# Scores, transposes and values of an attention part as bursts, the first score held until two banks are free

## The chip, the cores and the metric

The kernel runs on one core of a Trainium2 chip. The metric is the device time of one execution in microseconds, as the median of several runs.

## The reference

Two blocks of layers over a sequence of 256 rows of 1024 features, all in float32. The first block has two layers of a hybrid mixer (attention beside a state-space branch) and a feed-forward part. The second has four layers, each of two feed-forward parts around a mixer: sliding-window attention with sinks, attention with three branches, block attention, sliding-window attention again. Every mixer has attention of this form:

```python
s = jnp.einsum("bqgrd,bkgd->bgrqk", q_n, k_n).astype(jnp.float32) * scale + bias
p = masked_softmax(s, ok, sink)
o = jnp.einsum("bgrqk,bkgd->bqgrd", p.astype(v.dtype), v_n)
```

Heads have 64 features. Queries and keys stand in blocks of 128 rows; the later block sees both blocks of keys, the earlier one only its own.

## The kernel before

The 256 rows are two tiles of 128, t = 0 and t = 1. Weights stream from HBM, are split into a rounded part and a remainder by ScalarE and VectorE (lines 192, 193, 197, 198), and TensorE multiplies with three products each (lines 227 to 229 for projections, 245 to 247 for products with the rows of an output weight).

All attention goes through `attend`. It takes eight heads in two parts of four. The four heads of a part are named by `par` (0 or 1) and `i` (0 or 1); `par` says in which half of the 128 partitions the head's 64 features lie. A part does the following.

- Scores, line 638: a matmul of 64 rows for each `i`, each block of keys `kt` (one for t = 0, two for t = 1) and each `par`. The heads of `par` 0 go to the PSUM tile `s[0]`, those of `par` 1 to `s[1]`. Each takes a bank of the pool `acc`, which has two banks for each t. The same pool holds the projections of the mixers (`proj`) and the sums of the output product (`acc`), so a new `s` needs both banks of its t back from whatever stood there.
- Reductions with the bias on VectorE (line 646), exponentials on ScalarE (line 649), the divisor (lines 653 to 658), the scaling of the weights of attention (lines 660 and 661).
- Transposes of the attention weights on TensorE (line 669), four to a bank: for t = 0 one bank holds both `par`, for t = 1 each `par` has its own. A copy brings them to SBUF (line 672 on VectorE or 674 on ScalarE).
- Values, line 680: matmuls of 64 columns, `par` 0 to the upper half of the partitions of one bank, `par` 1 to the lower.

The order of the instructions on each engine isn't that of the program text. A scheduler takes, for each engine, the instruction of the lowest priority number among those that it finds ready, by its own estimates; the engines then work their lists in order, with semaphores between them. Numbers go up by one with each instruction, and `pr` sets where a block of work begins: the second tile's work lies `lag` units of weights behind the first's. So the matmuls of lines 638, 669 and 680 are mixed with projections and output products wherever their banks or operands come free one by one.

Six stretches of the program have attention: the hybrid layers (two parts for each t), the two sliding-window mixers and the block mixer C (four), and the mixer B with its two branches of full attention (eight).

Of the kernel before, what the change touches and what calls it, by code (L numbers as in the profile page):

```python
# [17 lines left out]
P = 128  # L18
# [83 lines left out]
class Program:  # L102
# [29 lines left out]
    @contextmanager  # L132
    def pr(self, t, first=0):


        tc = self.tc
        at = int(1000 * (self.unit + {0: 0, 1: self.lag, 2: -PREP}[t] - first))
        key = t, first
        keep, tc.cur_priority = tc.cur_priority, 20000 + max(at, self.at.get(key, 0))
        try:  # L140
            yield
        finally:
            self.at[key] = tc.cur_priority - 20000
            tc.cur_priority = keep

    def btile(self, t, shape, dtype=F32, name="b"):
        return self.wp.tile(shape, dtype, name=f"{name}{t}", tag=f"b{t}", bufs=NB)
# [475 lines left out]
    def attend(self, t, q, k, v, bias, out, sink=None, gate=None, parts=(0, 1)):  # L623

        nc = self.nc
        nk = (t + 1) * P
        four = lambda a: a.rearrange("p (i r) -> p r i", r=2)
        for part in parts:  # L630
            heads = slice(4 * part, 4 * part + 4)
            m, den, rden = (self.small(t, [P, 2, 2], n) for n in ("m", "den", "rden"))
            s = [self.acc(t, (P, 2, 256), "s") for _ in range(2)]
            for i in range(2):
                for kt in range(t + 1):
                    for par in range(2):
                        h = 4 * part + par + 2 * i
                        nc.tensor.matmul(s[par][:, i, kt * P:(kt + 1) * P], q[64 * par:64 * par + 64, h // 2],  # L638
                                         k(h, kt), start=True, stop=True)
            e = [self.btile(t, [P, 2, 256], name="e") for _ in range(2)]  # L640
            for par in range(2):
                for i in range(2):
                    h = 4 * part + par + 2 * i
                    ei = e[par][:, i, :nk]
                    init = BIG if sink is None else sink[1][:, h:h + 1]
                    nc.vector.tensor_tensor_reduce(
                        out=ei, in0=s[par][:, i, :nk], in1=bias(h)[:, 256 - nk:256], scale=-0.125,
                        scalar=init, op0=OP.add, op1=OP.min, accum_out=m[:, par, i:i + 1])
                    nc.scalar.activation(ei, ei, AF.Exp, scale=-1.0, bias=m[:, par, i:i + 1],
                                         accum_out=den[:, par, i:i + 1])  # L650
            if sink is not None:
                z = self.small(t, [P, 2, 2], "sk")
                nc.vector.tensor_add(z, four(sink[0][:, heads]), m)
                nc.scalar.activation(z, z, AF.Exp)
                nc.vector.tensor_add(den, den, z)
            nc.vector.reciprocal(rden, den)
            if gate is not None:
                nc.vector.tensor_mul(rden, rden, four(gate[:, heads]))
            for i in range(2):
                nc.scalar.activation(e[0][:, i, :nk], e[0][:, i, :nk], AF.Identity, scale=rden[:, 0, i:i + 1])  # L660
            nc.vector.tensor_mul(e[1][:, :, :nk], e[1][:, :, :nk], rden[:, 1, :, None].to_broadcast([P, 2, nk]))
            pts = {}
            step = 2 - t
            for par in range(0, 2, step):
                tp = self.bank(t, (P, step, 2, t + 1, P), "tp")
                for r in range(step):
                    for i in range(2):
                        for kt in range(t + 1):
                            nc.tensor.transpose(tp[:, r, i, kt], e[par + r][:, i, kt * P:(kt + 1) * P], self.ident)  # L669
                pt = self.wp.tile([P, step, 2, t + 1, P], F32, name=f"pt{t}", tag=f"pt{t}", bufs=2)  # L670
                if (par if t else part):
                    nc.vector.tensor_copy(pt, tp)
                else:
                    nc.scalar.activation(pt, tp, AF.Copy)
                pts.update({par + r: pt[:, r] for r in range(step)})
            pv = self.bank(t, (P, 2, P), "pv")
            for i in range(2):
                for kt in range(t + 1):
                    for par in range(2):
                        nc.tensor.matmul(pv[64 * par:64 * par + 64, i], v(4 * part + par + 2 * i, kt),  # L680
                                         pts[par][:, i, kt], start=(kt == 0), stop=(kt == t))
            out(part, pv)

    def stationary(self, t, tag="X", n=4):
# [233 lines left out]
    def do_B(self, i, j):  # L918
# [19 lines left out]
        def c():  # L938
            Wc = self.columns(W, [(1024, 512)])
            for u in range(2):  # L940
                pr = self.btile(0, [16, P], name="pr")
                nc.sync.dma_start(pr, A["b_cmp_pos_2"][j, u].rearrange("(k i) d -> k (i d)", i=2))
                tp = self.bank(0, (P, 16), "tp")
                nc.tensor.transpose(tp, pr, self.ident[:16, :16])
                ptile = bp.tile([P, 16], F32, name=f"pos{u}")
                nc.vector.tensor_copy(ptile, tp)
                pos.append(ptile)
                w = bp.tile([P, 2, 2, 64], F32, name=f"cw{u}")
                for e in range(2):
                    nc.sync.dma_start(w[:, :, e], A["b_cmp_w2_2"][j, u].rearrange("(k p) n -> p k n", p=P))  # L950
                w2.append(w)
            for t in range(NT):
                with self.pr(t):
                    ps = self.project(t, X[t], Wc, 512)
                    for u in range(2):
                        self.compress_source(t, ps[:, u * 256:(u + 1) * 256], raw[:, u])
# [350 lines left out]
```

## Time and profile before

| | |
|---|---|
| median of 3 runs | 2733.43 us (2732.55 to 2736.84) |
| the profiled execution | 2739.28 us, span 2737.5 us |
| TensorE busy | 2673.5 us, 98% |
| VectorE busy | 1796.9 us, 66% |
| ScalarE busy | 1547.4 us, 57% |
| GpSimd busy | 96.3 us, 4% |
| granted TensorE clock, mean | 0.995 |

Busy time of TensorE is the time in which at least one matmul is under way; matmuls overlap, and their ends are modelled. How much of the engine's time a matmul takes is therefore read from the starts of rows that follow each other. The chain of work that ended last lies on TensorE for 79% of the span. A matmul with full float32 operands, such as those of lines 638 and 680, leaves two records, a transpose and a projection one.

### The profile page before, as it was taken

How to read it: one execution, taken by the hardware profiler on the slowest of the kernel's cores; microseconds unless marked ns; L12 is line 12 of the kernel's file. 1: busy time of each engine (PE TensorE's matmuls, PEld its weight loads, DVE VectorE, ACT ScalarE, POOL GpSimd, SP SyncE). 2: the span in 40 equal slices, each digit the busy share in tenths (PEclk: the TensorE clock that was granted, in tenths of full speed). 3: DMA queues.
4: the chain of work that ended last, by engine and by line, in shares of the span. 5: the costliest groups of instructions: out<-in, count | busy, mean ns of one | idle time of the engine just before them, and what ended most of it. 6: DMA issues, size and time to landing. Idle time of an engine off the chain costs nothing.

```text
span 2737.5 us, 36688 instructions
## 1 busy us (share of the span) xinstructions
PE 2673.5 (98%) x12883; PEld 2141.6 (78%) x12883; DVE 1796.9 (66%) x3466; ACT 1547.4 (57%) x2893; POOL 96.3 (4%) x102
## 2 busy tenths in 40 slices
PE   8999999999999999999999999999999999999998
PEld 6678787778788778878877778788777788887787
DVE  8866668776665676576557766666566656657764
ACT  6645546565554565565455655555576555547653
POOL 0300002100000000000000000000000000000000
PEclk9999999999999999999999999999999999999999
DMA  6357742566566346555552266565546656553662
GB/s 208 102 165 207 214 131 88 172 218 188 179 190 195 117 161 203 189 185 185 184 185 81 80 213 188 175 199 185 162 139 187 200 175 196 189 166 112 208 192 85
DMA packets 338277, 465.18 MB, mean 170 GB/s; under 512 B 27780, under 2 KB 273196, under 8 KB 338092
## 3 DMA queue, kind: packets, MB, share of 16 engines
q1 hardware_dynamic: 336512, 460.49, 53.8%
q10 hardware_dynamic: 1580, 2.35, 0.5%
q8 instruction: 101, 1.65, 0.3%
q14 instruction: 84, 0.69, 0.1%
HBM read 460.13 MB, written 2.62 MB: 169 GB/s over the span
## 4 chain that ended last, share of the span: by engine, by line
PE 79%; DVE 8%; DMA 6%; ACT 3%; issue 2%; POOL 1%; SPq 0%; ACTq 0%; DVEq 0%; POOLq 0%
PE proj L227 15%; PE proj L229 15%; PE proj L228 15%; PE acc L245 8%; PE acc L247 8%; PE acc L246 8%; PE s L638 3%; DMA stage<-in_ffn_w_in 2%; PE tp L254 2%; DVE slot L198 2%; DVE slot L193 2%; PE pv L680 2%; DMA stage<-in_w_up 2%; PE tp L669 1%; ACT slot L197 1%
## 5 line engine op out<-in xcount | busy, mean ns | idle before, releaser
L198 DVE SCALAR_TENSOR_TENSOR slot<-stage,gt,slot 128x512 fp32r<-128x512 f32 (+2 forms) x1024 | 710.4, 740 | 339.7 <-ACT slot L197 338.8
L197 ACT ACTIVATE slot<-stage,gt 128x512 fp32r<-128x512 f32 (+2 forms) x1024 | 677.2, 710 | 409.8 <-PE proj L229 199.7
L227 PE MATMUL proj<-slot,X 128*128 128x512 f32 (+2 forms) x2272 | 897.2, 395 | 10.7 <-DVE X L257 8.8
L229 PE MATMUL proj<-slot,X 128*128 128x512 f32 (+2 forms) x2272 | 883.3, 389 | 0.0
L228 PE MATMUL proj<-slot,X 128*128 128x512 f32 (+2 forms) x2272 | 882.5, 388 | 0.0
L227 PEld LDWEIGHTS proj<-slot,X 128*128 128x128 f32 x2272 | 428.1, 189 | 101.7 <-DVE X L257 13.0
L229 PEld LDWEIGHTS proj<-slot,X 128*128 128x128 f32 x2272 | 428.0, 188 | 86.5 <-issue 0.9
L193 DVE TENSOR_TENSOR slot<-stage,slot 128x1024 fp32r<-128x1024 f32 (+1 forms) x330 | 406.6, 1235 | 134.5 <-ACT slot L192 131.2
L228 PEld LDWEIGHTS proj<-slot,X 128*128 128x128 f32 x2272 | 428.9, 189 | 79.8 <-issue 1.3
L192 ACT ACTIVATE slot<-stage 128x1024 fp32r<-128x1024 f32 (+1 forms) x330 | 346.9, 1054 | 166.7 <-DMA stage<-in_ffn_w_out 66.0
L245 PE MATMUL acc<-slot,H 128*128 128x512 f32 x880 | 353.5, 402 | 4.6 <-ACT H L256 4.6
L247 PE MATMUL acc<-slot,H 128*128 128x512 f32 x880 | 344.3, 392 | 1.8 <-DVE H L257 1.7
L246 PE MATMUL acc<-slot,H 128*128 128x512 f32 x880 | 343.3, 390 | 0.0
L504 ACT ACTIVATE th<-proj,r 128x256 f32<-128x256 f32 x220 | 103.7, 472 | 296.7 <-PE proj L229 273.9
L506 DVE SCALAR_TENSOR_TENSOR h<-th,proj 128x256 f32<-128x256 f32 x220 | 91.8, 417 | 208.5 <-ACT th L504 208.4
L247 PEld LDWEIGHTS acc<-slot,H 128*128 128x128 f32 x880 | 165.1, 188 | 41.4 <-DVE H L257 5.8
L245 PEld LDWEIGHTS acc<-slot,H 128*128 128x128 f32 x880 | 165.3, 188 | 39.6 <-ACT H L256 9.2
L246 PEld LDWEIGHTS acc<-slot,H 128*128 128x128 f32 x880 | 165.7, 188 | 31.5
L257 DVE TENSOR_TENSOR H<-tp,H 128x256 fp32r<-128x256 f32 x220 | 92.1, 419 | 33.2 <-ACT H L256 32.8
L256 ACT ACTIVATE H<-tp 128x256 fp32r<-128x256 f32 x220 | 83.0, 377 | 39.6 <-PE tp L254 39.5
L507 DVE SCALAR_TENSOR_TENSOR h<-h,r,proj 128x256 f32<-128x256 f32 x220 | 104.0, 473 | 0.7
L278 POOL TENSOR_TENSOR rstd<-rstd,mhalf 128x1 f32<-128x1 f32 x34 | 29.1, 855 | 2130.8 <-DVE rstd L273 2067.7
(219 smaller groups left out, 2169.5 us busy)
## 6 DMA issues: line engine op xcount, KB each, us to landing
stage<-in_ffn_w_in SPq DMA_DIRECT2D x704, 256.0 KB, 3.9
stage<-in_ffn_w_out SPq DMA_DIRECT2D x176, 512.0 KB, 4.1
stage<-in_w_in SPq DMA_DIRECT2D x48, 512.0 KB, 3.8
stage<-in_w_gate SPq DMA_DIRECT2D x88, 256.0 KB, 3.8
stage<-in_w_up SPq DMA_DIRECT2D x88, 256.0 KB, 4.0
stage<-in_w_down SPq DMA_DIRECT2D x44, 512.0 KB, 4.5
stage<-in_w_out SPq DMA_DIRECT2D x24, 512.0 KB, 3.7
stage<-in_c_w_in SPq DMA_DIRECT2D x24, 512.0 KB, 4.4
```

What stands on the lines that cost most here:

```text
L192: nc.scalar.activation(r[:, 0], s[:, i:i + step], AF.Copy)
L193: nc.vector.tensor_sub(r[:, 1], s[:, i:i + step], r[:, 0].bitcast(F32))
L197: nc.scalar.activation(r[:, 0, j], s[:, i + j], AF.Identity, scale=gk)
L198: nc.vector.scalar_tensor_tensor(r[:, 1, j], s[:, i + j], gk, r[:, 0, j].bitcast(F32), op0=OP.mult, op1=OP.subtract)
L227: mm(ps, x[0], w[1], start=start, stop=False)
L228: mm(ps, x[0], w[0], start=False, stop=False)
L229: mm(ps, x[1], w[0], start=False, stop=stop)
L245: mm(acc[j], a[0], wl, start=start and i == 0, stop=False)
L246: mm(acc[j], a[0], wh, start=False, stop=False)
L247: mm(acc[j], a[1], wh, start=False, stop=stop and i == n - 1)
L504: nc.scalar.activation(th, pg[:, 0:256], AF.Tanh, scale=self.r_half[t])
L507: nc.vector.scalar_tensor_tensor(h, h, self.r_square[t], pg[:, 256:512], op0=OP.mult, op1=OP.mult)
```

## The change

`burst` emits a list of calls. The first keeps its place in the order of priorities and may depend on an instruction given as `after`; the others get numbers lower by 10000 and are bound to program order, so that they follow the first as soon as the scheduler finds them ready. It is used for the scores, the transposes and the values.

For the scores, a memset of one element of `s[1]` on VectorE is made first, and the first score, which writes `s[0]`, depends on it. The memset itself can only run when the bank of `s[1]` is free. The scores' loop changes from `i, kt, par` to `kt` (falling), `i, par`. The transposes of t = 0 begin with `par` 1. In the values, `par` 1 comes ahead of `par` 0, so that the first value is one that needs the copy made last.

```diff
+    def burst(self, calls, after=None):
+        tc = self.tc
+        keep = tc.cur_priority
+        for i, (f, args, kw) in enumerate(calls):
+            ins = f(*args, **kw)
+            if i == 0:
+                if after is not None:
+                    tc.add_manual_dep(ins.ins, after.ins.name, mybir.DependencyInfo(
+                        mybir.DependencyClass.Sync, mybir.DependencyReason.DATA), reason="both banks")
+                tc.cur_priority -= 10000
+            else:
+                tc.keep_in_program_order(ins)
+        tc.cur_priority = keep + len(calls)
...
             s = [self.acc(t, (P, 2, 256), "s") for _ in range(2)]
-            for i in range(2):
-                for kt in range(t + 1):
-                    for par in range(2):
-                        h = 4 * part + par + 2 * i
-                        nc.tensor.matmul(s[par][:, i, kt * P:(kt + 1) * P], q[64 * par:64 * par + 64, h // 2],
-                                         k(h, kt), start=True, stop=True)
+            held = nc.vector.memset(s[1][0:1, 0, 0:1], 0.0)
+            self.burst([(nc.tensor.matmul, (s[par][:, i, kt * P:(kt + 1) * P],
+                                            q[64 * par:64 * par + 64, 2 * part + i], k(4 * part + par + 2 * i, kt)),
+                         dict(start=True, stop=True))
+                        for kt in range(t, -1, -1) for i in range(2) for par in range(2)], held)
...
-                for r in range(step):
-                    for i in range(2):
-                        for kt in range(t + 1):
-                            nc.tensor.transpose(tp[:, r, i, kt], e[par + r][:, i, kt * P:(kt + 1) * P], self.ident)
+                self.burst([(nc.tensor.transpose, (tp[:, r, i, kt], e[par + r][:, i, kt * P:(kt + 1) * P],
+                                                   self.ident), {})
+                            for r in range(step - 1, -1, -1) for i in range(2) for kt in range(t + 1)])
...
-            for i in range(2):
-                for kt in range(t + 1):
-                    for par in range(2):
-                        nc.tensor.matmul(pv[64 * par:64 * par + 64, i], v(4 * part + par + 2 * i, kt),
-                                         pts[par][:, i, kt], start=(kt == 0), stop=(kt == t))
+            self.burst([(nc.tensor.matmul, (pv[64 * par:64 * par + 64, i], v(4 * part + par + 2 * i, kt),
+                                            pts[par][:, i, kt]), dict(start=(kt == 0), stop=(kt == t)))
+                        for i in range(2) for kt in range(t + 1) for par in (1, 0)])
```

In the rows of the order below, the number behind a name tells its tiles apart. TensorE's order at the first scores of t = 1 in the first sliding-window mixer, before: `s1_8447` is `s[0]` of the first part and `s1_8448` its `s[1]`, `s1_8503` is `s[0]` of the next part, and `proj1` and `tp1` belong to a projection of the same tile.

```order
L229 MATMUL proj1_8327<-slot_8289,X1_8062 128x512
L638 MATMUL s1_8447<-slot_8084,slot_8085 128x128
L638 MATMUL s1_8447<-slot_8085 128x128
L638 MATMUL s1_8447<-slot_8084,slot_8085 128x128
L638 MATMUL s1_8447<-slot_8085 128x128
L265 MATMUL tp1_8354<-c1_81,cp1_8352 128x128 x4
L638 MATMUL s1_8448<-slot_8084,slot_8085 128x128
L638 MATMUL s1_8448<-slot_8085 128x128
L638 MATMUL s1_8448<-slot_8084,slot_8085 128x128
L638 MATMUL s1_8448<-slot_8085 128x128
L638 MATMUL s1_8503<-slot_8084,slot_8085 128x128
```

The same place of TensorE's order now, where `s1_8457` and `s1_8458` are the two banks of the first part:

```order
L280 MATMUL tp1_8362<-c1_81,cp1_8360 128x128 x4
L151 MATMUL s1_8457<-slot_8093 128x128
L151 MATMUL s1_8458<-slot_8093 128x128
L151 MATMUL s1_8457<-slot_8093 128x128
L151 MATMUL s1_8458<-slot_8093 128x128
L151 MATMUL s1_8457<-slot_8092,slot_8093 128x128
L151 MATMUL s1_8458<-slot_8092,slot_8093 128x128
L151 MATMUL s1_8457<-slot_8092,slot_8093 128x128
L151 MATMUL s1_8458<-slot_8092,slot_8093 128x128
L262 MATMUL acc0_8808<-slot_8770,X0_8568 128x512
```

The four scores of one bank and, behind a transpose, the four of the other have become one run of eight that alternates between the banks, and the next part's scores no longer stand behind it.

TensorE's order at the values of the second part of t = 1, a little later in the same mixer, before (`acc0` is the output product of the other tile, `pt1` the copied transposes):

```order
L246 MATMUL acc0_8792<-slot_8764,X0_8556 128x512
L680 MATMUL pv1_8545<-pt1_8536,slot_8084 64x128
L247 MATMUL acc0_8792<-slot_8764,X0_8556 128x512
L245 MATMUL acc0_8793<-slot_8764,X0_8556 128x512
L680 MATMUL pv1_8545<-pt1_8543,slot_8084 64x128
L680 MATMUL pv1_8545<-pt1_8536,slot_8085 64x128
L680 MATMUL pv1_8545<-pt1_8543,slot_8085 64x128
L680 MATMUL pv1_8545<-pt1_8536,slot_8084 64x128
L680 MATMUL pv1_8545<-pt1_8543,slot_8084 64x128
L680 MATMUL pv1_8545<-pt1_8536,slot_8085 64x128
L680 MATMUL pv1_8545<-pt1_8543,slot_8085 64x128
L246 MATMUL acc0_8793<-slot_8764,X0_8556 128x512
```

The values of the same part now, with the last score of a later part ahead of them:

```order
L151 MATMUL s1_8715<-slot_8092,slot_8093 128x128
L151 MATMUL pv1_8557<-pt1_8555,slot_8092 64x128
L151 MATMUL pv1_8557<-pt1_8548,slot_8092 64x128
L151 MATMUL pv1_8557<-pt1_8555,slot_8093 64x128
L151 MATMUL pv1_8557<-pt1_8548,slot_8093 64x128
L151 MATMUL pv1_8557<-pt1_8555,slot_8092 64x128
L151 MATMUL pv1_8557<-pt1_8548,slot_8092 64x128
L151 MATMUL pv1_8557<-pt1_8555,slot_8093 64x128
L151 MATMUL pv1_8557<-pt1_8548,slot_8093 64x128
L261 MATMUL acc0_8808<-slot_8795,X0_8368 128x512
```

The lone value and the seven behind two output products have become one run of eight.

VectorE's order in the same mixer, around the first part's reductions of t = 1, now (`e1`, `m1`, `sk1` and `den1` are the part's own, `slot` and `stage` are weights):

```order
L660 ISA e1_8469,m1_8454<-s1_8458,bias_8078,nsink_8090 128x256
L660 ISA m1_8454 128x1
L649 MEMSET s1_8515 1x1
L208 TENSOR_TENSOR slot_8800<-stage_8798,slot_8800 128x1024
L667 TENSOR_TENSOR sk1_8478<-sink_8088,m1_8454 128x4
L208 TENSOR_TENSOR slot_8805<-stage_8803,slot_8805 128x1024
L669 TENSOR_TENSOR den1_8455<-den1_8455,sk1_8478 128x4
L660 ISA e1_8525,m1_8511<-s1_8514,bias_8078,nsink_8090 128x256
```

The memset of the next part stands right behind the last reduction of this part; before, the next part's first reduction stood there, with its scores already made.

## Rows read from the trace of the kernel before

**Rows 1.** Page: busy us (share of the span) and instructions of each engine.

```profile
PE 2673.5 (98%) x12883; PEld 2141.6 (78%) x12883; DVE 1796.9 (66%) x3466; ACT 1547.4 (57%) x2893; POOL 96.3 (4%) x102
```

**Rows 2.** Stretches, length, then busy PE, PEld, DVE, ACT, POOL (instructions); clock, DMA.

```profile
1468.00:1551.00 83.00, 82.78 (x607) 61.66 (x607) 62.39 (x235) 59.62 (x189) 0.00 (x0) 1.00 0.15 46
934.00:990.00 56.00, 55.92 (x358) 41.09 (x357) 39.20 (x127) 40.68 (x121) 0.00 (x0) 1.00 0.32 103
2008.00:2060.00 52.00, 51.96 (x346) 39.02 (x345) 33.13 (x106) 37.15 (x107) 0.00 (x0) 1.00 0.36 111
...
57.00:111.00 54.00, 49.69 (x283) 36.35 (x281) 49.31 (x123) 38.03 (x91) 16.80 (x13) 1.00 0.31 93
415.00:469.00 54.00, 49.85 (x290) 36.82 (x288) 49.54 (x123) 38.34 (x90) 16.08 (x13) 1.00 0.30 92
```

**Rows 3.** Waits of PE, 55 to 112 us: us in total, times, longest.

```profile
PE s L638 <- DVE m L646: 1.6, 1, 1.6
```

**Rows 4.** Timeline of PE, 57 to 68 us: start, us, engine, line, operation, records.

```profile
56.90 0.39 PE L229 MATMUL proj<-slot,X 128*128 128x512 f32 x1
57.22 0.71 PE L638 MATMUL s<-slot 64*128 64x128 f32 x4
57.86 0.50 PE L227 MATMUL proj<-slot,X 128*128 128x512 f32 x1
58.20 0.39 PE L228 MATMUL proj<-slot,X 128*128 128x512 f32 x1
...
66.97 0.72 PE L638 MATMUL s<-slot 64*128 64x128 f32 x8
67.61 0.50 PE L227 MATMUL proj<-slot,X 128*128 128x512 f32 x1
```

**Rows 5.** Timeline of all engines, 957 to 976 us: four scores of one bank.

```profile
957.53 1.16 PE L638 MATMUL s<-slot 64*128 64x128 f32 x8
...
958.62 0.66 PE L265 MATMUL tp<-c,cp 128*128 128x128 f32 x4
```

**Rows 6.** Timelines of PE at 70, 100 and 980 us: values together and split.

```profile
70.80 0.66 PE L680 MATMUL pv<-pt,slot 128*64 128x128 f32 x8
...
100.67 1.09 PE L680 MATMUL pv<-pt,slot 128*64 128x128 f32 x16
...
979.47 0.43 PE L680 MATMUL pv<-pt,slot 128*64 128x128 f32 x2
979.83 0.50 PE L246 MATMUL acc<-slot,X 128*128 128x512 f32 x1
...
980.49 1.09 PE L680 MATMUL pv<-pt,slot 128*64 128x128 f32 x14
981.51 0.50 PE L245 MATMUL acc<-slot,X 128*128 128x512 f32 x1
```

**Rows 7.** Stretches, instructions of line 638 (scores) alone: busy PE and PEld.

```profile
1468.00:1551.00 83.00, 30.02 (x192) 21.83 (x192) 1.00 0.15 46
934.00:990.00 56.00, 13.92 (x96) 10.86 (x96) 1.00 0.32 103
2008.00:2060.00 52.00, 12.63 (x96) 10.14 (x96) 1.00 0.36 111
...
57.00:111.00 54.00, 7.25 (x48) 5.55 (x48) 1.00 0.31 93
415.00:469.00 54.00, 6.42 (x48) 5.14 (x48) 1.00 0.30 92
sum 355.00, PE 84.16 PEld 64.37; mean PE 14.03 PEld 10.73
```

**Rows 8.** The same for line 680 (values), sum of the six stretches.

```profile
sum 355.00, PE 51.84 PEld 34.70; mean PE 8.64 PEld 5.78
```

**Rows 9.** Groups by form on VectorE, 1465 to 1552 us: busy, mean ns, idle before.

```profile
L646 DVE DVE_READ_ACCUMULATOR2_ANT m<- 128x1 f32 x64 | 5.3, 83 | 0.0
```

**Rows 10.** Instructions of line 344: ns minimum, median and maximum, start.

```profile
L344 DVE MEMSET mhalf<- x1: 59/59/59, 0.8 to 0.8; 128x1 f32 x1
```

## Prediction

> **What bounds the kernel now.** I read the busy shares first. TensorE (PE) is busy 98% of the span [rows 1], so the question is whether PE works to full effect in the places that the change touches. These are the six attention stretches: one in each of the two hybrid layers, two sliding-window mixers, the mixer with two attention branches (B), and the block mixer (C). The table of stretches [rows 2] shows two kinds. In B, C and the sliding-window mixers (934 to 990; its twin, the same mixer of a later layer, is alike) PE has no idle time worth naming, while the vector engine (DVE) is busy 75%, 64% and 70% and ScalarE (ACT) 72%, 71% and 73%. There the end moves if PE's work gets less. In the two hybrid stretches (57 to 111 and 415 to 469) DVE is busy 91 and 92% and PE waits some 4 us in all, for instance 1.6 us for one score that wanted a bank whose reductions were still running [rows 3]. There less work for PE buys little.
>
> Then the timeline of PE, by starts of neighbouring rows. Each score or value matmul leaves two records, so x4 is two matmuls. Full-size projections follow each other every 0.23 us. Two scores of the same bank sit between projections that start at 56.90 and 57.86, then 58.20 [rows 4]: the score starts 0.32 us after the projection before it (0.09 more than usual), runs 0.64, and the second projection behind it comes after 0.34 (0.11 more). Entering and leaving the half-height scores therefore costs time of its own. Four scores that alternate between the two banks take 0.72 us busy (66.97, next row at 67.61); four scores of one bank take 1.16 (957.53) [rows 4, 5]. Alternating scores use the two halves of the array at once, and before, this is rare: the list of scores mostly has runs of one bank, since each bank comes free on its own. Values show the same: all eight of a second-tile part together take 1.09 (100.67), but split they are 0.43 and again 1.09, with projections between (979.47 and 980.49) [rows 6]. The lone first value is one whose copy came first.
>
> **The change part by part.** Counts are of the order on PE. There are 48 parts, 24 of the first tile (4 scores, 4 values) and 24 of the second (8 and 8): 2 of each kind in a hybrid stretch, 4 in a sliding-window mixer or in C, 8 in B. Scores stand in 103 runs before and 47 after, nearly all of 4 or 8, always alternating. Values stand in 71 runs before (23 lone ones) and 48 after. Entries to such work from full-size work go from 140 to 75, by stretch: B 46 to 21, sliding-window 25 to 12 (twice), C 18 to 14, hybrids 14 and 12 to 8.
>
> Scores: a first-tile part takes 0.72 [rows 4]; a second-tile part has four more pairs, which by the values cost 1.09 - 0.66 = 0.43 [rows 6], so 1.15. Per pair of parts 1.87. Against the busy time of the scores [rows 7]: B 30.0 to 8 x 1.87 = 15.0, saving 15.0; a sliding-window mixer 13.9 to 7.5, saving 6.4; C 12.6 to 7.5, saving 5.1; the hybrids 7.25 and 6.42 to 3.7, saving 3.5 and 2.7. All: 84.2 to 45, saving 39.
>
> Two scores on two halves of the array are not free of each other here: 0.72 for four paired against 1.16 unpaired is a factor of 1.6 [rows 4, 5]. The Trainium skill, TensorEngine Tiling (Array Packing), section Theoretical Speedup, allows up to 2 for a small dimension of at most 64. By that factor the four would take 0.58, eight about 1.0, and the scores would save some 7 us more, which would put the time near 2689; the row has the entry in it, and the row decides.
>
> Values: 24 x 0.66 + 24 x 1.09 = 42.0 against 51.8 [rows 6, 8] saves 9.8, or 0.41 per pair of parts: B 3.3, the mixers of four 1.6 each, the hybrids 0.8 each.
>
> Entries and exits: 0.09 + 0.11 less the 0.07 by which a run's busy time reaches past the next start (57.22 + 0.71 against 57.86) leaves 0.13 [rows 4]. 65 fewer: 8.5 us, of which B 3.3, sliding-window 1.7 each, C 0.5, hybrids 0.8 and 0.5.
>
> Transposes: their runs go from 96 to 69. They are full-size work like the projections around them, so no entry to half the array is saved. I take nothing for them; at the 0.09 that an entry costs, 27 runs would be 2.4 us either way.
>
> The hold: 48 memsets of one element on DVE. The trace has one small memset of 0.059 us on a column of 128 in SBUF [rows 10]; none of PSUM, so I bound it by that and by the 0.083 us of the accumulator read, the shortest frequent step of the same loop [rows 9]. On DVE's queue the weight remainders and the other tile's reductions stand behind it. In the order shown for the sliding-window mixer it stands right behind the last reduction of the bank it waits for, so the queue does not stop for it there. Its price on the path is one memset between the last read of the bank and the first score: 48 x 0.06 = 2.9 us if nothing covers it, 0 if PE has projections to do, as it mostly has. Beyond that the hold takes from the first bank the head start it had: before, its scores could run while the second bank was still being reduced. For this the stretches without PE idle show no price. One side is 0; on the other stands the hybrid's 1.6 us wait [rows 3], taken per part. I take the 2.9, near the low end, because a part's first score no longer has to be early: DVE has other tiles' and weights' work while the burst runs.
>
> PE's sum by stretch: B 15.0 + 3.3 + 3.3 = 21.6; sliding-window 6.4 + 1.6 + 1.7 = 9.7, twice; C 5.1 + 1.6 + 0.5 = 7.2; hybrids 5.1 and 4.0. Together 57.3.
>
> What is late next: DVE and ACT do the same work in less time. The busiest that DVE gets in any attention stretch is the 91% of the first hybrid stretch [rows 2]; I take this as what it can reach. B: 62.4 + 16 memsets of 0.07 = 63.5, over 0.913 = 69.5 us, against 83 - 21.6 = 61.4 for PE. So B gains 13.5, not 21.6. A sliding-window mixer: DVE 39.7 over 0.913 = 43.5, PE 46.3, ACT 40.7 (88% of it): PE still sets it, gain 9.7. C: PE 44.8, DVE 33.7 over 0.913 = 36.9, ACT 83%: gain 7.2. The hybrids already stand at that share: gain 0. Sum 13.5 + 19.4 + 7.2 = 40.1, less 2.9 for the memsets: 37 us. What stands outside these stretches (feed-forward blocks) gets the same work in the same order.
>
> The profiled execution took 2739.28 us, 5.85 above the median of 2733.43. 2739.28 - 37 = 2702.3 is the like of it; on the median, 2733.4 - 37 = 2696.4.
>
> **The rivals.** (1) The whole of PE's saving arrives: 57.3, 2676. It needs DVE to be as good as full in B, or to move B's weight remainders out of it. For it: PE, not DVE, ends the waits in B now. Against: DVE's work there is longer than PE's new time. The Trainium skill, TensorEngine Tiling (Array Packing), section PSUM Bottleneck, says that tiling speeds up TensorE but not the emptying of PSUM, which may then be the bound. That speaks against this rival, and its effect in B is in my sum as DVE's floor. (2) The hold makes a chain: with both banks bound together, a part's reductions, exponentials and transposes start later, and PE runs out of projections. At half the hybrid's wait, 0.8 us per part, 48 x 0.8 = 38 of 57.3 is lost: 18 or 19 saved, 2715. For it: in the second half of B the order has little full-size work left between the bursts. Against: PE does not wait in these stretches now. (3) Slower: the same chain at full price, every burst waiting as the hybrid's score did. 48 x 1.6 = 77 against 57.3 is 20 us slower, 2753. It decides from 57.3 / 48 = 1.2 us a part. (4) The pairs do not run together (the second bank's scores start only after the first's): only entries and exits are saved, 8.5 us, 2725. Against: the run at 66.97 is this very order and pairs.
>
> **How the numbers follow.** Forecast 0.66, (1) 0.12, (2) 0.12, (3) 0.05, (4) 0.05. About 0.2%, 5.5 us, is what a measurement of this kernel can tell from no change. The forecast, (1), (4) and most of (2) are faster by more: 0.90. Between (2) and (3) lies no change, 0.05 with what (2) leaves; slower 0.05. The range goes from the whole saving, 2675, to rival (2) with its rounding, 2717; outside it are (3), (4) and a little of (2), under 2 in 10.
>
> **What would show it.** Right: score runs of 8 and 16 records with 0.7 and 1.15 us, scores' busy time near 45 and values' near 42; no lone values; B shorter by some 13 us with DVE above 88% in it, the sliding-window mixers by 9 or 10 each, C by 7, the hybrids unmoved; PE's busy time in all down by more than the span. New waits of PE for DVE in B are the sign that DVE's floor binds; waits at the first score of a burst, behind a memset, are the sign of (2) or (3). Scores that stay at 1.1 us for eight records mean (4). The prediction is wrong if the hybrids get longer, or if feed-forward blocks lose what the mixers gain because weights come late.

## The result and the profile after

The changed kernel takes 2704.42 us (median of four runs, 2700.56 to 2706.00), the kernel before 2732.99 in the same comparison: ratio 0.9887, interval 0.9872 to 0.9902. By the ratio that is 31 us less, by the two medians 28.6; 37 were forecast. Line numbers of after are higher by 11 to 15, and all bursts are recorded on line 151.

The page's busy times and the head of its chain:

```profile
PE 2624.0 (97%) x12883; PEld 2106.8 (78%) x12883; DVE 1796.5 (66%) x3514; ACT 1544.8 (57%) x2893; POOL 94.3 (3%) x102
PE 73%; DVE 9%; DMA 7%; ACT 5%; issue 2%; POOL 1%; SPq 0%; ACTq 0%; DVEq 0%; POOLq 0%
```

Against [rows 1], TensorE (PE) is busy 49.5 us less and VectorE (DVE) and ScalarE (ACT) the same; the span fell by 34.6 (2737.5 to 2702.9). That is more than the medians show, because the profiled execution of before was 5.85 us above its median. So some 15 us of what PE no longer does became idle time of PE.

What the change was made of came out as forecast. PE's timeline of after (start, busy, tiles, records):

```profile
929.74 0.72 PE L151 MATMUL s<-slot 64*128 64x128 f32 x8
950.00 1.16 PE L151 MATMUL s<-slot 64*128 64x128 f32 x16
1475.20 0.66 PE L151 MATMUL pv<-pt,slot 128*64 128x128 f32 x8
1496.28 1.09 PE L151 MATMUL pv<-pt,slot 128*64 128x128 f32 x16
```

Eight records are four scores, as in [rows 4, 5]. The scores' and then the values' busy time, as sums over the six attention stretches of after, and the hold's memset:

```profile
sum 366.00, PE 45.97; mean PE 7.66
sum 366.00, PE 42.88; mean PE 7.15
L649 DVE MEMSET s<- x48: 59/59/59, 52.0 to 2481.1; 1x1 f32 x48
```

45.97 and 42.88 stand against 84.16 [rows 7] and 51.84 [rows 8]; 45 and 42.0 were forecast. Part of the small excess is a lower clock in B, which is shown below.

Where it went shows when the program is cut at the residual additions that end each block. A row has start and end, length, busy time of each engine, PE's granted clock and the share of the DMA engines. Six blocks with attention, of before, then of after (the two hybrid layers, sliding-window, B, C, sliding-window):

```profile
0.00:183.20 183.20, 164.85 (x831) 127.75 (x832) 146.69 (x366) 111.17 (x215) 29.41 (x27) 0.99 0.50 156
377.20:540.90 163.70, 152.66 (x781) 118.06 (x780) 131.94 (x286) 98.25 (x190) 27.57 (x22) 0.99 0.43 131
923.70:1011.60 87.90, 86.81 (x510) 66.16 (x510) 64.13 (x172) 61.47 (x160) 3.85 (x4) 1.00 0.40 129
1396.70:1576.80 180.10, 178.55 (x1076) 135.81 (x1076) 124.81 (x350) 108.05 (x282) 2.58 (x4) 0.98 0.39 119
1959.70:2083.20 123.50, 122.93 (x670) 95.92 (x669) 81.19 (x184) 82.79 (x184) 2.55 (x4) 1.00 0.49 152
2463.50:2550.70 87.20, 86.64 (x510) 66.24 (x510) 64.15 (x171) 61.42 (x159) 2.58 (x4) 1.00 0.41 130
```

```profile
0.00:180.10 180.10, 160.96 (x831) 125.08 (x832) 144.67 (x370) 110.30 (x214) 27.54 (x27) 0.99 0.52 158
372.90:534.40 161.50, 149.96 (x784) 115.55 (x783) 131.25 (x290) 98.60 (x189) 28.05 (x22) 0.99 0.44 134
916.60:999.50 82.90, 79.20 (x513) 61.53 (x513) 63.85 (x180) 60.03 (x159) 2.57 (x4) 1.00 0.44 138
1380.40:1554.50 174.10, 163.25 (x1080) 126.38 (x1079) 125.25 (x365) 107.29 (x283) 3.56 (x4) 0.96 0.40 125
1933.40:2052.30 118.90, 116.85 (x671) 90.97 (x669) 81.76 (x192) 81.99 (x184) 2.54 (x4) 1.00 0.50 157
2432.70:2516.90 84.20, 79.52 (x513) 61.36 (x513) 63.87 (x179) 60.69 (x160) 3.47 (x4) 1.00 0.43 135
```

| block | PE busy less | length less | forecast for it |
|---|---|---|---|
| hybrid layers | 3.9, 2.7 | 3.1, 2.2 | 0, 0 |
| sliding-window, first | 7.6 | 5.0 | 9.7 |
| B | 15.3 | 6.0 | 13.5 |
| C | 6.1 | 4.6 | 7.2 |
| sliding-window, last | 7.1 | 3.0 | 9.7 |
| feed-forward blocks together | | about 11 | 0 |

So the attention blocks gave 24 us, not 40, and the feed-forward blocks gave 11 that nobody forecast: 4.2 in the one behind the first sliding-window mixer, 4.0 in the one behind B, the rest in small pieces. Their work is unchanged. The head of the one behind the first sliding-window mixer, before and after, and PE's longest wait in the head of before (us, times, longest):

```profile
1011.60:1036.00 24.40, 21.66 (x94) 17.66 (x95) 15.89 (x29) 14.18 (x26) 0.92 (x1) 0.93 0.67 213
999.50:1024.00 24.50, 23.56 (x110) 19.33 (x111) 19.20 (x34) 17.44 (x31) 0.55 (x1) 1.00 0.76 234
PE proj L227 <- DVE X L257: 2.6, 1, 2.6
```

Before, PE waited 2.6 us for the block's first input and its clock then fell (0.93 in the mean of that stretch); after, the same wait is 0.5 and the clock 1.00. The block behind B reads the same (2.5 us and 0.93 before, 0.2 us and 1.00 after). The two blocks took 193.6 us each before, 189.4 and 189.6 after. The kernels below that have one kind of burst alone, all at full clock in these two blocks, tell what this goes with: 189.2 and 189.5 with the scores' bursts alone, 192.9 and 190.4 with the transposes' alone. So in the first block the gain comes with the scores' bursts; in the second a kernel without them has most of it too. Why the input comes sooner was not tried.

In B something new happens. PE's timeline of after between 1478 and 1493, with the idle time ahead of a row and who ended it, and below it rows of stretches as above:

```profile
1478.60 1.92 PE L151 MATMUL s<-slot 64*128 64x128 f32 x24
1481.35 0.63 PE L151 MATMUL tp<-c,e 128*128 128x128 f32 x4 [0.82 <-ACT e L663]
1482.76 0.66 PE L151 MATMUL pv<-pt,slot 128*64 128x128 f32 x8 [0.79 <-DVE pt L685]
1484.84 1.01 PE L151 MATMUL pv<-pt,slot 128*64 128x128 f32 x8 [0.83 <-DVE m L660]
1487.81 2.08 PE L151 MATMUL s<-slot 64*128 64x128 f32 x16
1492.13 0.80 PE L260 MATMUL acc<-slot,X 128*128 128x512 f32 x1 [1.19 <-ACT X L1034]
```

```profile
1481.50:1484.70 3.20, 1.72 (x16) 1.07 (x15) 3.10 (x16) 3.20 (x13) 0.00 (x0) 1.00 0.55 164
1488.00:1491.50 3.50, 2.94 (x24) 2.31 (x24) 2.32 (x6) 0.06 (x1) 0.00 (x0) 0.50 0.55 159
```

The projections are used up by 1478; the output product starts at 1492, when ScalarE's X is there. Between them PE has only the parts' own chain (scores, reductions, exponentials, transposes, copies, values) and waits at each link. Up to 1484.7 VectorE and ScalarE are as good as full (the first of the two rows); later they are not. From 1484.7 PE's clock stands at its lower level (0.50, 1.2 GHz) for 10.2 us; sixteen records of scores then take 2.08 us instead of 1.16.

This is not the only fall of the clock in B. After has another of 3.4 us at 1430 (0.89 in the mean of 1425 to 1440), and before had one of 6.8 us, from 1443.9, with PE busy throughout:

```profile
1443.70:1450.50 6.80, 6.80 (x25) 4.91 (x25) 4.52 (x13) 2.12 (x5) 0.00 (x0) 0.52 0.29 85
```

So neither B of the table is at full clock. By the sixteen records (2.08 against 1.16) 6.8 us at the lower level cost some 3.0: without its fall, B of before would have taken some 177.1 us, with PE busy for 175.5 (both estimates, from these rows and the block's).

### The profile page after: what moved, and what is told of

Same layout as the page of the kernel before. It is cut to its first block, busy times and chain, and to the rows that moved or that the text cites. A ratio compares the mean times of both kernels' runs of the same rounds, so it can differ in the third digit from the quotient of the medians.

```text
span 2702.9 us, 36766 instructions
## 1 busy us (share of the span) xinstructions
PE 2624.0 (97%) x12883; PEld 2106.8 (78%) x12883; DVE 1796.5 (66%) x3514; ACT 1544.8 (57%) x2893; POOL 94.3 (3%) x102
## 4 chain that ended last, share of the span: by engine, by line
PE 73%; DVE 9%; DMA 7%; ACT 5%; issue 2%; POOL 1%; SPq 0%; ACTq 0%; DVEq 0%; POOLq 0%
PE proj L242 15%; PE proj L244 15%; PE proj L243 15%; PE acc L260 7%; PE acc L262 7%; PE acc L261 7%; DVE slot L213 3%; PE tp L269 2%; DMA stage<-in_ffn_w_in 2%; DVE slot L208 2%; DMA stage<-in_w_up 1%; ACT slot L212 1%; ACT slot L207 1%; DMA stage<-in_w_down 1%; PE tp L151 1%
## 5 line engine op out<-in xcount | busy, mean ns | idle before, releaser
L293 POOL TENSOR_TENSOR rstd<-rstd,mhalf 128x1 f32<-128x1 f32 x34 | 28.6, 840 | 2100.0 <-DVE rstd L288 2039.7
```

## The experiments

Ratios are against the kernel before; the changed kernel stands at 0.9887, and an interval is about 0.0015 (4 us) to either side. Differences in us are taken from the ratios (0.001 is 2.7 us). First the three kinds of bursts one at a time, the rest as before.

**Scores alone.**

```diff
# transposes and values: loops as before
+            held = nc.vector.memset(s[1][0:1, 0, 0:1], 0.0)
+            self.burst([... scores, alternating ...], held)
```

> Scores as held bursts alone; transposes and values as before. Theory (the pairing of scores carries most of the gain): scores' busy time falls from 84 to 46 us, entries to half-array work from 140 to 90; some 45 of the 57 us of the sum for PE stay, and the time is 22 to 28 us under before, ratio 0.990 to 0.992. Rival (the gain comes from whole values and fewer entries as much as from pairs): 10 to 14 us, ratio near 0.996.

Measured 2711.66 us, 0.9913 (0.9898 to 0.9928), scores 46.89: 24 us less. As the theory had it.

**Values alone.**

```diff
+            self.burst([... values, par 1 ahead of par 0 ...])
```

> Values as bursts alone, the copy made last first; scores and transposes as before. Theory: values' busy time 51.8 to 42.9 us, 18 fewer entries at 0.13; 8 to 12 us under before, ratio 0.9955 to 0.997. Rival (a value that waits for the last copy holds PE and gives it back): ratio 0.999 to 1.001.

Measured 2721.42, 0.9950 (0.9935 to 0.9966), values 42.05: 14 us less, above the 8 to 12 of the theory, whose nearest ratio (0.9955) lies inside the interval.

**Transposes alone.**

```diff
+                self.burst([... transposes, par 1 first ...])
```

> Transposes as bursts alone. Theory: no gain from the transposes themselves, 15 fewer entries at 0.13 is 2 us; ratio 0.999 to 1.0005. Rival (transposes between projections cost about 0.1 us each): 22 fewer runs give another 2 us, and holding the first transpose until both of its inputs are there may cost as much.

Measured 2730.18, 0.9985 (0.9974 to 0.9996): 4 us less, at the edge of what can be told and just under the theory's range; the 2 us more that the rival names would fit, but the interval reaches both. The three add up to 42 us, the whole is 31: they share part of their gain.

**Scores and values, transposes as before.**

```diff
-                self.burst([... transposes ...])
+                for r in range(step): ... nc.tensor.transpose(...)
```

> The changed kernel with the transposes as they were before: bursts of scores (held) and of values only. The entries into work on half the array stay at 76 by the order of instructions, against 75. Theory (the three parts share one saving, since alone they gave 23.8, 13.7 and 4.1 us and together only some 30): with scores and values in, the bursts of transposes bring nothing more, the time is that of the changed kernel within 3 us, ratio 0.987 to 0.990. Rival (each part keeps its own gain and the sum is cut elsewhere): the 4 us of the transposes are lost again, ratio 0.9900 to 0.9915.

Measured 2699.83, 0.9874 (0.9856 to 0.9893). The theory holds: behind the other two, bursts of transposes bring nothing that can be measured. This is the fastest median of all, but its interval overlaps that of the changed kernel, so it is not shown to be better.

**No hold.**

```diff
-            held = nc.vector.memset(s[1][0:1, 0, 0:1], 0.0)
...
-                        for kt in ... for par in range(2)], held)
+                        for kt in ... for par in range(2)])
```

> The changed kernel without the small write: the first score is free to go as soon as the first bank is, before the second bank is free. By the order of instructions TensorE's scores then fall apart in most parts into one and three (or seven), and the entries into work on half the array rise from 75 to 120. Theory (the hold pays): a lone score is a pass of some 0.35 to 0.4 us with nothing beside it, so the scores' busy time rises from 46 to 50 to 56 us, the entries cost another 45 x 0.13 = 6 us, and the wait for the second bank stands on TensorE again in the midst of a burst; part of it is hidden behind VectorE and ScalarE. Time 3 to 10 us above the changed kernel, ratio to the kernel before 0.990 to 0.993. Rival (the hold buys nothing, since the second bank is free by then): within 2 us of the changed kernel, ratio 0.988 to 0.9895, scores below 48 us. Second rival (the hold costs): faster than the changed kernel, ratio below 0.988.

Measured 2720.82, 0.9946 (0.9932 to 0.9959): 16 us above the changed kernel, more than the 3 to 10 of the theory. Its scores in a sliding-window mixer, and their sum:

```profile
936.07 0.48 PE L151 MATMUL s<-slot 64*128 64x128 f32 x2
937.31 0.71 PE L151 MATMUL s<-slot 64*128 64x128 f32 x6
952.53 1.16 PE L151 MATMUL s<-slot 64*128 64x128 f32 x14
sum 366.00, PE 68.28; mean PE 11.38
```

The lone first score costs 0.48, and the three behind it take the 0.71 that four would: the odd partner runs beside nothing. 48 x 0.48 = 23 us of scores, against my 4 to 10. With bursts as they are, half of the change's gain depends on the hold.

**Bank by bank.** The hold stays; all scores of the first bank, then all of the second.

```diff
-                        for kt in range(t, -1, -1) for i in range(2) for par in range(2)], held)
+                        for par in range(2) for kt in range(t, -1, -1) for i in range(2)], held)
```

> The changed kernel with its hold, but a burst makes all scores of the first bank and then all of the second. Theory (two scores run at once only when neighbours in the order lie on different halves of the array): scores' busy time back to 70 to 77 us, entries stay at 78; the time lies 12 to 18 us under before, ratio 0.9935 to 0.9955. Rival (unbroken runs and fewer entries bring the gain, not the alternation): the ratio of the changed kernel, 0.9887.

Measured 2704.02, 0.9890 (0.9874 to 0.9906): no different from the changed kernel, a miss; the ratio is the rival's. One reason is in the scores:

```profile
931.41 0.72 PE L151 MATMUL s<-slot 64*128 64x128 f32 x8
949.74 1.71 PE L151 MATMUL s<-slot 64*128 64x128 f32 x16
```

Two scores of one bank and then two of the other take no longer than alternating ones, and four and four take 1.71 instead of 1.16: PE begins the other half's matmuls though some of the first half stand ahead of them. The scores sum to 58.98 us, a third of the way back to 84: two thirds of the saving are there without alternating. Those 13 us more did not show in the time, so what the alternation itself is worth is not shown; what this kernel shares with the changed one is unbroken runs with both banks free. Block B took 167.7 us instead of 174.1: it has the fall of the clock of 3.4 us at 1430, but not the one of 10.2. The feed-forward block behind it took 193.5 instead of 189.6. The next kernel does it in B alone.

**Bank by bank in B alone.**

```diff
+                        for (kt, i, par) in (bank by bank if gate is not None else alternating)], held)
```

> The changed kernel with the scores of B alone issued bank by bank (all of the first bank, then all of the second, the hold kept); all other mixers alternate banks. Theory (in B TensorE is not the bound, and the first bank's scores ready a little sooner help VectorE's chain): the scores of B rise from 15.9 to some 19.7 us and the time does not: 0 to 5 us below the changed kernel, ratio 0.987 to 0.989, and block B from the last add to its own last add at 167 to 174 us, against 174.1 in the changed kernel's profile. Rival (TensorE's time counts in B, and the short block of the kernel that goes bank by bank everywhere was its clock in that execution): 3 to 5 us above the changed kernel, ratio 0.990 to 0.991, block B at 174 to 178 us.

Measured 2707.65, 0.9897 (0.9883 to 0.9911). The time decides nothing: it lies between the two ranges, 3 us above the changed kernel, and the interval reaches both. Block B took 168.9, as the theory said (with one fall of the clock of 3.4 us), and the feed-forward block behind it took 192.9 instead of 189.6. The same 16 us around its start, here and in the changed kernel:

```profile
1548.00:1564.00 16.00, 13.42 (x57) 10.46 (x56) 12.27 (x23) 9.49 (x19) 2.38 (x2) 0.89 0.69 212
1548.00:1564.00 16.00, 15.34 (x72) 12.28 (x71) 14.11 (x26) 12.04 (x23) 2.09 (x2) 1.00 0.72 236
```

The clock fell there instead (0.89 in the mean of the stretch). This kernel's block B ended 3 us sooner, so the two rows are not the same work to the instruction.

**What a microsecond of VectorE costs.** One spare multiply a part, in B, and then in the two sliding-window mixers.

```diff
+            if gate is not None:      # the other kernel: sink
+                spare = self.wp.tile([P, 2, 256], BF, name="spare", tag="spare", bufs=1)
+                nc.vector.tensor_mul(spare[:, :, :nk], e[1][:, :, :nk], e[1][:, :, :nk])
```

> The changed kernel with one spare VectorE multiply of each part's second e tile in the gated mixer B alone (16 parts, by the rows of the same multiply some 9 us of VectorE in all; its result is read by nothing). Theory (in B the changed kernel is bound by VectorE and ScalarE, not TensorE): most of it shows, 6 to 10 us above the changed kernel, ratio 0.991 to 0.993. Rival (B is short of the forecast only because TensorE's clock fell there for 10 us, and TensorE is the bound): VectorE has 86.0 - 68.8 = 17 us of room in the stretch, and the multiplies cost 0 to 3 us, ratio 0.9885 to 0.990.

> The changed kernel with the same spare VectorE multiply in the two sliding-window mixers instead of B (16 parts in all, the same size of tiles). Theory (there TensorE is the bound, at 62.4 of 65 us, and VectorE is busy for 49.2): 0 to 3 us above the changed kernel, ratio 0.9885 to 0.990. Rival (every mixer waits for VectorE's chain part by part, so a longer chain shows anywhere): 6 to 10 us, ratio 0.991 to 0.993, as much as in B.

They added 7.1 and 7.4 us to VectorE's busy time. Measured 2707.24, 0.9896 (0.9882 to 0.9909), in B and 2708.90, 0.9899 (0.9883 to 0.9916), in the sliding-window mixers: 2.5 and 3.3 us above the changed kernel, which is inside the intervals. In B the rival holds: block B is 174.2 us long with the multiplies and 174.1 without, at the same mean clock (0.96), so VectorE is not what is full there. The sliding-window blocks took 85.7 and 84.1 us against 82.9 and 84.2: nearer to the theory than to the rival's 6 to 10.

**What a microsecond of TensorE costs.** Every score of B, and then of the sliding-window mixers, computed twice.

```diff
+                        for _ in range(1 if gate is None else 2)      # the other kernel: sink
                         for kt in range(t, -1, -1) for i in range(2) for par in range(2)], held)
```

> The changed kernel with every score of the gated mixer B computed twice (the second time over the first, in the same burst): some 16 us more of TensorE in B and nothing more for another engine. It prices a microsecond of TensorE there as the spare multiplies priced one of VectorE (0.3). Theory (in B TensorE is short of work for part of the block, where VectorE and ScalarE set the pace, and the clock falls there): part of the 16 us goes into the holes, and the clock's fall near 1485 goes too, 4 to 10 us above the changed kernel, ratio 0.9902 to 0.9925. Rival (TensorE is the bound in B after all): 13 to 17 us, ratio 0.9935 to 0.995.

> The changed kernel with every score of the two sliding-window mixers computed twice, some 15 us more of TensorE in the two. Theory (there TensorE is the bound, busy for 62.4 of 65 us): 11 to 15 us above the changed kernel, ratio 0.993 to 0.994. Rival (the same price as in B, or less): 4 to 9 us, ratio 0.990 to 0.992.

The second scores add 0.9 us to sixteen records, so both kernels add less than I wrote: 10.9 us in B, 5.4 in each sliding-window mixer. In B: 2707.05, 0.9894 (0.9876 to 0.9913), 2 us above the changed kernel. That is under the theory's range of 4 to 10; the clock's fall is gone, as it said, 1.00 through all of B:

```profile
1381.70:1557.20 175.50, 167.28 (x1272) 133.14 (x1271) 125.93 (x365) 108.01 (x282) 3.47 (x4) 1.00 0.40 123
```

In the sliding-window mixers: 2716.43, 0.9934 (0.9918 to 0.9951), 13 us above. Their two blocks and, below, block B of this second kernel, where nothing is changed:

```profile
918.30:1008.90 90.60, 83.93 (x608) 66.48 (x607) 66.59 (x181) 62.44 (x161) 2.57 (x4) 1.00 0.43 130
2437.50:2527.70 90.20, 83.54 (x606) 66.23 (x606) 65.81 (x179) 61.12 (x159) 2.57 (x4) 1.00 0.42 126
1391.80:1559.00 167.20, 157.50 (x1080) 122.61 (x1079) 124.83 (x365) 106.17 (x281) 2.56 (x4) 1.00 0.42 129
```

The sliding-window blocks grew by 7.7 and 6.0 us for 4.7 and 4.0 more of PE's busy time, and PE's idle time in them grew too (3.7 to 6.7, 4.7 to 6.7). So the theory's number came true, but not because PE is full there. Scores stand at the head of each part's chain, and a longer head may delay all that follows; this was not tried by itself.

Block B is what I had not looked for. Around its gap the timeline shows the order and the waits of the changed kernel again, 8 us later, at full clock:

```profile
1486.69 1.92 PE L151 MATMUL s<-slot 64*128 64x128 f32 x24
1489.43 0.63 PE L151 MATMUL tp<-c,e 128*128 128x128 f32 x4 [0.82 <-ACT e L664]
1490.84 0.66 PE L151 MATMUL pv<-pt,slot 128*64 128x128 f32 x8 [0.78 <-DVE pt L686]
1492.93 0.66 PE L151 MATMUL pv<-pt,slot 128*64 128x128 f32 x8 [0.85 <-DVE m L661]
1495.10 1.16 PE L151 MATMUL s<-slot 64*128 64x128 f32 x16
1498.40 0.50 PE L260 MATMUL acc<-slot,X 128*128 128x512 f32 x1 [1.53 <-ACT X L1035]
```

B took 167.2 us here, PE 157.5 of them, against 174.1 and 163.25, and the clock fell nowhere in it. Same work, same order in the gap, same waits up to the point where the clock fell. The changed kernel's profile had 13.6 us of B at the lower level (3.4 and 10.2), which by the same two rows (2.08 against 1.16) cost some 6.0: that is the 5.8 us of PE's time and most of the 6.9 us of length by which the two differ.

This also corrects the reading of the kernel with B's scores doubled. Against an undisturbed B of 167.2 us, those scores cost 8.3 us of the 10.9 they add; they look nearly free only against a B in which the clock fell. Going bank by bank in B, with 6.8 us more of PE's time (164.26 against 157.50, some 1.5 of it for 3.4 us at the lower clock), made it only 1.7 us longer. So what PE's time costs in B depends on where it is spent.

**Values twice near the gap**, to see whether more work for PE there keeps the clock up.

```diff
+                        for _ in range(2 if t and gate is not None and self.first else 1)
                         for i in range(2) for kt in range(t + 1) for par in (1, 0)])
```

> The changed kernel with the values of four parts computed twice, the second time over the first: the second tile's first half of the gated mixer B, which runs in the stretch where TensorE is short of work and where its clock fell (about 1480 to 1500). It adds some 4 us of TensorE there, at the end of each part's chain, where the next part's scores don't wait for it. Theory (B fell short by the clock, which falls because TensorE stands idle there a quarter of the time): with less idle time the clock of that stretch stays at 1.00, B is 167 to 171 us instead of 174.1, and the kernel is 0 to 5 us faster than the changed kernel though it does more, ratio 0.9865 to 0.9885. Rival (the added work costs what it takes, and the clock falls anyway): 2 to 5 us slower than the changed kernel, ratio 0.9895 to 0.9905, the granted clock of 1478 to 1500 below 0.9.

Measured 2707.55, 0.9897 (0.9880 to 0.9913): the time is in the rival's range. Block B took 170.1, the clock was 1.00, as the theory wanted. But it does not decide: the added values landed from 1493 on, behind the gap, and the gap itself stood as it was:

```profile
1484.90 0.66 PE L151 MATMUL pv<-pt,slot 128*64 128x128 f32 x8 [0.84 <-DVE m L660]
1490.37 0.50 PE L260 MATMUL acc<-slot,X 128*128 128x512 f32 x1 [1.53 <-ACT X L1036]
1493.06 1.97 PE L151 MATMUL pv<-pt,slot 128*64 128x128 f32 x32
```

So the same gap is on record a third time, and for the second time at full clock. The gap alone does not settle whether the clock falls. Of the nine profiles with bursts of alternating scores in B, five show the lower clock somewhere between 1478 and 1505 (the changed kernel, scores alone, no hold, both with spare multiplies) and four do not; neither of the two with B bank by bank does. What tells these apart was not found.

## Why the prediction was right, and where it was not

The time (2696.4) was 6 us under what the ratio gives on the same median (2733.4 x 0.9887 = 2702.5) and 8 under the median measured, and the range held it. That the sum came so close is in good part luck: no block came out as forecast (the table above). The attention blocks gave 24 us where 40.1 were forecast, the feed-forward blocks 11 where nothing was. By its steps:

- **Pairs, values, counts: right.** 0.72, 0.66 and 1.09 came as forecast, 1.16 for 1.15, and the sums within 1 us of 45 and 42. Rival (4) is refuted.
- **PE's sum: too high by the entries.** At full clock B's PE time fell from 175.5 (the estimate above) to 157.5, 18.0 against 21.6. In the sliding-window mixers it fell 7.6 and 7.1 against 9.7. Scores and values alone make 18.8 in B (30.0 to 15.0, 17.9 to 14.0) and 8.1 in a sliding-window mixer (13.9 to 7.5, 8.7 to 7.0). So the 3.3 and 1.7 for entries did not show there; 0.13 an entry, taken at one place, doesn't hold.
- **PE's whole saving arrives in the sliding-window mixers and C: wrong.** This is the step that failed. 3.0 to 5.0 of 6.1 to 7.6 arrived. I had a floor only by VectorE's busy share, and found none there. What was missing is the chain from engine to engine: PE idled 1.1 us in the first such mixer before and 3.7 after, 0.6 and 4.7 in the last. The waits are named in the profile of after, over the whole span:

```profile
PE tp L151 <- ACT e L674: 6.3, 7, 1.8
PE pv L151 <- DVE pt L685: 2.7, 7, 0.8
PE s L151 <- DVE s L649: 1.0, 2, 0.8
```

- **The hybrids gain 0: wrong, the other way.** They gained 3.1 and 2.2 us of PE's 3.9 and 2.7. VectorE's share there, 91% (and 92% in the second, which the prediction passed over in calling 91% the most it gets), was no bound. That shorter scores shorten the chain on which PE waits would explain it; no run tried it.
- **VectorE's 91% bounds B: size too high, reason wrong.** At full clock B gives 177.1 - 167.2 = 9.9 us, where 13.5 was forecast. And 7 us more of VectorE's work made the kernel 2.5 us longer, not 7, VectorE was busy for only 70.67 us of the 86 around the gap (82%, where more than 88% was to be the sign) in the undisturbed B, and PE's longest idle times in B end on ScalarE as well as VectorE. PE idles 9.7 us of the undisturbed B, against 1.5 before; 5.1 of them lie between 1486 and 1499, in the gap between projections and output product where only parts' chains are left. This gap is the picture of rival (2), which saw that B has little full-size work between the bursts; its price per part was too high.
- **The clock: not in the sum.** B stood at the lower clock for 13.6 us after and 6.8 before, some 3.0 us lost by the estimates above, and two feed-forward blocks gave back 8 us that a wait and a fall of the clock at their heads had taken before. Neither was forecast. With the 5.3 us of the hybrids, the feed-forward blocks' 11 cover most of what B, C and the sliding-window mixers fell short by (21.5).
- **The hold's price, 2.9 us: at most that.** PE's waits behind the memset are the last row above and two like it, 3 us in all, some of it on weight loads. Rivals (2) and (3), 0.8 and 1.6 us a part, would be 38 and 77. What the prediction left out is the gain: without the hold 16 us are lost again.
- **Transposes at nothing: right within the whole**, though alone they gave 4 us.

## What to carry to other kernels

An engine busy 98% of a stretch is a bound only until its work is cut: ask which chain of the other engines runs beside it. Here 40 to 80% of what PE's busy time fell by arrived in each of the six blocks. Look for the place where the filler work (here projections) runs out first; that is where the new idle time opens, and the work behind it may run at a lower clock, as it did here in five of nine profiles. If two banks must be free for a paired run, wait for both once, ahead of the run: here, without that, scores took some 22 us more (68.28 against 45.97) and the kernel 16. And read the granted clock of both kernels before taking a difference of two blocks: B of before had lost some 3 us to it.

## What the runs showed of the hardware

Paired and unpaired scores fit a start and a step. Alternating: four take 0.72 us, eight 1.16, sixteen 2.06 (the kernel with B's scores doubled): 0.28 to start and 0.11 each. Of one bank: two take 0.71 and four 1.16 [rows 4, 5], 0.26 to start and 0.225 each, from these two alone; the lone score without the hold, 0.48, fits them. So a score in a paired run takes half the time, and only the start made my comparison of fours give 1.6. The Trainium skill, TensorEngine Tiling (Array Packing), section Theoretical Speedup, has up to 2 for a small dimension of at most 64; by the step from one length to the next the trace agrees (0.225 / 0.11), and the prediction's remark that the row spoke against it mixed the start in.

TensorE pairs some scores even when all of one bank stand first: 1.71 us for four and four, where unpaired ones would by this take 0.26 + 8 x 0.225 = 2.06 and alternating ones take 1.16.

The same gap, its first three waits the same to 0.02 us, was followed by 10.2 us of half clock in one profile and by none in two others.
